# The last gates of a gated five-branch mixer layer: loading W_out's blocks in four groups between the gates, in a new order of steps

## The chip, the cores and the metric

One core of one Trainium2 chip runs the whole program. The metric is device microseconds of one execution, as the median of several runs of the same program. All data is float32 in device memory; a profiled execution gives the trace that the sections below read. Engines are named as the profile names them: PE (TensorE's matmuls), PEld (its weight loads), DVE (VectorE), ACT (ScalarE), POOL (GpSimd), SP (SyncE, which here only issues DMAs), and PEq, SPq, POOLq, ACTq for the queues that issue.

## The reference, cut to what matters

For 512 tokens of width 1024 a layer computes a normalised input, one wide projection of it, five branches of width 512, and merges them by gates:

```python
h = rmsnorm(x, norm_g)
proj = h @ w_in + b_in                 # branch inputs, and 5 x 1024 gate logits
y_a, y_b, y_c, y_d, y_m = ...          # five branches, each (512 tokens, 512)
gates = jax.nn.sigmoid(gate_logits).reshape(b, s, N_BRANCH, D_MODEL)
merged = jnp.zeros_like(x)
for n, y in enumerate((y_a, y_b, y_c, y_d, y_m)):
    merged = merged + gates[:, :, n] * (y @ w_up[n])
x = x + merged @ w_out
return rmsnorm(x, final_norm_g)
```

Branch D (number 3) is a gated linear recurrence over the tokens; it is the last to be finished here, so its gates and its up-projections end the merge, and the product with `w_out` (1024 x 1024), the residual and the last norm follow.

## The kernel before, in words

**Arithmetic.** Every large product is made of three matmuls (`mm3`, L196 to L201): both operands are split into a rounded part and a remainder (names ending in H or `hi`, and L or `lo`), and hi*hi, hi*lo and lo*hi are summed in one PSUM bank. One unit of 128 output channels with 1024 inputs is 8 x 3 = 24 matmuls of 128x512; one with 512 inputs is 12.

**Weights.** All weights come through one ring of two staging buffers, `wst` (`WST = 2`), of 512 KB each. `load_w` (L150) issues the load on SP's queue and splits it in two halves: `whi` by ACT (L162), `wlo` by DVE (L163). `load_w_add` (L171), used for the gates, makes `wlo` without DVE: ACT writes the negated rounded value (L182), POOL issues a DMA that reads the same weights from memory once more and adds them (L183), and ACT writes `whi` (L184). So each gate moves 512 KB on SP's queue and twice 256 KB on POOL's. `whi` and `wlo` have six halves each. A staging buffer is free for the next load when ACT (and DVE) have read it, and SP issues in order, so a load whose buffer is not yet free holds up every DMA behind it on SP.

**Steps.** The order of the work is written by hand in two strings, `STEPS` and `ENDS`, that a loop hands to `step(s)`. `G3` is one gate of branch D: a load, 24 matmuls, a sigmoid on ACT (L961). `U3` is one up-projection: 12 matmuls, then DVE multiplies by the gate (L975) and adds into `merged` (L977); one weight load serves two of them. `dt` and `dn` are D's tiles and its scan; `dn1` makes the last two of the four `y` tiles that every `U3` needs. There are eight `G3` and eight `U3`. Below, "gate 5" is the fifth `G3`, and so on. A scheduler then places each engine's instructions, so neighbouring steps overlap.

**W_out.** `merged @ w_out` is done by a scheme with fewer products: sums and differences of the blocks of `w_out` (`w0` to `w3`, in `weights(i)`, L1081) and of `merged`. `wout[half, k]` are the four blocks 11, 21, 12 and 22, each in two units `u` of 512 KB. In `ENDS` of the kernel before, `w0` loads both units of block 11 and `w1` both units of block 21 through `wst` and splits them (`operand`, L1059: `woH` by ACT, `woL` by DVE, both in `split_sb`, L218). `w2` and `w3` each handle one unit of the combined blocks: they load `t1` (block 12) into a buffer of its own, block 11 *again* through `wst` to subtract it (`minus`, L1065), `t2` (block 22) into a buffer of its own, subtract `t1`, and load block 21 *again* to subtract `t2` and split the result. So twelve 512 KB loads. `t1`, `t2`, `woH`, `woL` lie in `epool`, which takes the memory that the branches leave at `mid.close()`; the last reader there is D's scan.

**x's rows.** For the residual the first 256 tokens of `x` are loaded into buffers of the `y` tiles (`xr`, L1074), at the place in the program where `ENDS` begins.

**The last products.** Seven products follow (`product`, L1130), each two PSUM banks (one from pool `pj`, one from `at`). `take` (L1142) adds a bank to a row, `finish` (L1150) squares, normalises and stores. The last one, `b22` on the first 256 tokens, is done for tokens 0 to 127 in one piece of 512 columns and for tokens 128 to 255 in two pieces of 256 columns (`halves=(1, 2)`), both in one bank.

The whole order of the stretch is held by SP's queue, by the two staging buffers, and by ACT, DVE and POOL, which each work strictly in order.

Of the kernel before, what the change touches and what calls it, by code (L numbers as in the profile page):

```python
# [70 lines left out]
G4 U4 az3 an0 G4 G0 ao0 bv0 az2 az1 bp1 G0 ao2 ao3 ao1 ba2 U4 cv1 ba1 G0 U0 U4 ba0 U0 bv1 U0  # L71
G0 cg0 U0 bp2 ba3 G0 bp3 G1 ba6 ba4 ba5 U0 ba7 U0 G0 G0 U0 U0 G1 G1 cp0 G1 G1 cv0 cp2 ch0
U1 U1 G1 cp1 ds0 U1 U1 G1 U1 ch1 U1 G2 ch2 G1 cn0 G2 U1 cp3 G2 U1 ch3 G2 cn1 dt1 U2 dt0
U2 U2 dn0 G2 G3 G2 U2 U2 dt2 G2 U2 dt3 G3 G2 U2 G3 dn1
"""
ENDS = """
U2 G3 w0 G3 w1 G3 w2 G3 U3 w3 U3 U3 U3 G3 U3 U3 U3 U3
"""


def build(ctx, tc, x, mem, memT, cols_d, rows_d, wcm, wbv, wcv0, wcv1, wmk, wmv, wup, wout, dw, fg, out):
# [65 lines left out]
    def f32(t):  # L147
        return t.bitcast(F32)

    def load_w(src, n, scale=None, stage=wpool):  # L150

        st = stage.tile([P, 1056], F32, tag="wst", name="wst", bufs=WST)
        nc.sync.dma_start(out=st[:, :n], in_=src)
        res = []
        m = n // 2
        for half in range(2):
            hi = wpool.tile([P, 576], F32R, tag="whi", name="whi", bufs=WHL)
            lo = wpool.tile([P, 576], F32R, tag="wlo", name="wlo", bufs=WHL)
            f = st[:, half * m:(half + 1) * m]
            with tc.high_priority(offset=PREP):  # L160
                if scale is None:
                    act(hi[:, :m], f, AF.Copy)  # L162
                    V.tensor_tensor(out=lo[:, :m], in0=f, in1=f32(hi[:, :m]), op=ALU.subtract)  # L163
                else:
                    act(hi[:, :m], f, AF.Copy, scale=scale)
                    V.scalar_tensor_tensor(out=lo[:, :m], in0=f, scalar=scale, in1=f32(hi[:, :m]),
                                           op0=ALU.mult, op1=ALU.subtract)
            res.append((hi, lo))
        return res

    def load_w_add(src, n):  # L171

        st = wpool.tile([P, 1056], F32, tag="wst", name="wst", bufs=WST)
        nc.sync.dma_start(out=st[:, :n], in_=src)
        res = []
        m = n // 2
        for half in range(2):
# [805 lines left out]
    def step(s):  # L983
# [42 lines left out]
            assert None not in ys[i]  # L1026
            up(i, ys[i])
        elif c == "w":
            st[s] = weights(i)
        else:  # L1030
            raise ValueError(s)

# [17 lines left out]
    def block(half, k, u, tag="wst"):  # L1050
# [2 lines left out]
            t = wpool.tile([P, 1056], F32, tag="wst", name="wst", bufs=WST)[:, :D]  # L1053
        else:
            t = epool.tile([P, D], F32, tag=tag, name=tag, bufs=2)
        nc.sync.dma_start(out=t, in_=wout[half, 2 * k + u])
        return t

    def operand(f):  # L1059
# [10 lines left out]
    xr, sums, quarter = [], {}, {}  # L1070
    for t in range(2):
        xr.append([ypool.tile([P, S], F32, tag=f"y{n}", name=f"xr{t}{n}") for n in "HL"])
        for n in range(2):
            nc.sync.dma_start(out=xr[t][n], in_=x[t * P:(t + 1) * P, n * S:(n + 1) * S])  # L1074
    lo_t, hi_t = slice(0, H2), slice(H2, S)
    t1, t2, n4 = [], [], []

    def weights(i):
        if i < 2:
            return [operand(block(0, i, u)) for u in range(2)]  # L1080
        u = i - 2  # L1081
        t1.append(block(1, 0, u, "t1"))
        minus(t1[u], t1[u], block(0, 0, u))
        t2.append(block(1, 1, u, "t2"))
        minus(t2[u], t2[u], t1[u])
        f = block(0, 1, u)
        n4.append(operand(minus(f, f, t2[u])))

    for s in ENDS.split():
        step(s)  # L1090
    b11, b21 = st["w0"], st["w1"]
    hst.close()
    rpool = ctx.enter_context(tc.tile_pool(name="rpool", bufs=1, side="right"))
    s2H, s2L = (rpool.tile([P, 4, S], F32R, name=n) for n in ("s2H", "s2L"))
# [33 lines left out]
    def product(ps, a, sl, b, begin, halves=(1, 1), done=None):  # L1128

        for t in range(2):  # L1130
            tsl = slice(sl.start + t * P, sl.start + (t + 1) * P)
            w = S // halves[t]
            for c in range(halves[t]):
                cs = slice(c * w, (c + 1) * w)
                for j in range(4):
                    wh, wl = (v[:, (j % 2) * S + c * w:(j % 2) * S + (c + 1) * w] for v in b[j // 2])
                    ah, al = (v[:, j, tsl] for v in a)
                    mm3(ps[t][:, cs], [(ah, al, wh, wl)], first=begin and j == 0, last=j == 3, check=True)
                if done:
                    done(t, cs)  # L1140

# [72 lines left out]
    for t in range(2):  # L1214
        take(2 + t, 0, X[t])
        finish(2 + t, 0)
        take(2 + t, 1, X[t])
    Y = banks()
    product(Y, (s4H, s4L), hi_t, T1, True)
    for t in range(2):  # L1220
        take(2 + t, 1, Y[t])
        finish(2 + t, 1)

    def c12(t, cs):
        take(t, 1, Y[t], cs)
        finish(t, 1, cs)

    product(Y, (s4H, s4L), lo_t, b22, False, halves=(1, 2), done=c12)


def _layout(a):
# [56 lines left out]
```

## Time and profile before

| | us |
|---|---|
| median of 3 runs (860.98 to 866.45) | 862.5 |
| the profiled execution, its own time | 863.77 |
| its span in the profile | 862.1 |
| PE busy in the span | 829.0 |
| DVE busy | 601.7 |
| ACT busy | 499.6 |
| stretch between the last matmul of gate 4 and the first matmul of the `w_out` products | 742.2 to 812.97 |
| mean granted clock of the core | 0.987 |

The profile's lines are read so. The slice rows divide the span into 40 parts of 21.55 us; each digit is a share in tenths. A row of the timeline gives the start, the duration, the engine, the line, the operation, what it writes from what it reads, and in brackets how long its engine had been idle and what ended that. A matmul's duration is longer than its distance to the next, since matmuls are pipelined: the distance of two starts is the cost. The chain of waits in the end (PE 79%, issue 11%, DVE 4%, ACT 3%, DMA 2%) is PE for most of the program, so what PE waits for, and at what clock it runs, is what the end hangs on. DMA rows of a window give the count, the size and the median time from issue to landing.

### The profile page before, as it was taken

How to read it: one execution, taken by the hardware profiler on the slowest of the kernel's cores; microseconds unless marked ns; L12 is line 12 of the kernel's file. 1: busy time of each engine (PE TensorE's matmuls, PEld its weight loads, DVE VectorE, ACT ScalarE, POOL GpSimd, SP SyncE). 2: the span in 40 equal slices, each digit the busy share in tenths (PEclk: the TensorE clock that was granted, in tenths of full speed). 3: DMA queues.
4: the chain of work that ended last, by engine and by line, in shares of the span. 5: the costliest groups of instructions: out<-in, count | busy, mean ns of one | idle time of the engine just before them, and what ended most of it. 6: DMA issues, size and time to landing. Idle time of an engine off the chain costs nothing.

```text
span 862.1 us, 11382 instructions
## 1 busy us (share of the span) xinstructions
PE 829.0 (96%) x4028; PEld 697.3 (81%) x4028; DVE 601.7 (70%) x1136; ACT 499.6 (58%) x898; POOL 107.2 (12%) x159
## 2 busy tenths in 40 slices
PE   8999999999999999999999999999999999578995
PEld 7788888888898988888888988888888888356874
DVE  4879998997465597775647777487585645426796
ACT  6635475445645465666555464774659768633354
POOL 0000020101100241024322000110102011010010
PEclk9999999999999999999999999999999999879999
DMA  9442373544534333446534333652625456765232
GB/s 360 141 141 74 103 146 94 143 124 124 124 111 112 86 109 98 104 116 135 135 91 106 123 110 113 154 137 88 157 74 128 121 143 149 240 178 158 79 98 98
DMA packets 37712, 110.52 MB, mean 128 GB/s; under 512 B 4244, under 2 KB 4372, under 8 KB 37656
## 3 DMA queue, kind: packets, MB, share of 16 engines
q1 hardware_dynamic: 24952, 86.21, 30.2%
q0 software_dynamic: 11840, 22.03, 15.3%
q10 hardware_dynamic: 864, 1.57, 0.5%
q8 instruction: 31, 0.51, 0.2%
q14 instruction: 25, 0.20, 0.1%
HBM read 107.68 MB, written 2.11 MB: 127 GB/s over the span
## 4 chain that ended last, share of the span: by engine, by line
PE 79%; issue 11%; DVE 4%; ACT 3%; DMA 2%; POOL 1%; POOLq 0%; SPq 0%; ACTq 0%
PE pj L201 21%; PE pj L200 21%; PE pj L199 21%; DMA wlo<-in 2%; PE pj L530 2%; PE pj L529 2%; PE pj L528 2%; POOL wlo L183 1%; PE po L642 1%; PE wb L628 1%; PE og L833 1%; PE mk L286 1%; PE zb L599 1%; PE zb L598 1%; DMA mt<-in 1%
## 5 line engine op out<-in xcount | busy, mean ns | idle before, releaser
L201 PE MATMUL pj<-hH,wlo 128*128 128x512 f32 x768 | 303.0, 394 | 11.1 <-DMA wlo<-in 10.8
L199 PE MATMUL pj<-hH,whi 128*128 128x512 f32 x768 | 302.3, 394 | 8.4 <-ACT whi L184 8.4
L200 PE MATMUL pj<-hL,whi 128*128 128x512 f32 x768 | 302.1, 393 | 0.0
L162 ACT ACTIVATE whi<-wst 128x512 fp32r<-128x512 f32 (+1 forms) x172 | 106.9, 631 | 169.2 <-PE pj L200 117.3
L201 PEld LDWEIGHTS pj<-hH,wlo 128*128 128x128 f32 x768 | 145.7, 190 | 43.6 <-DMA wlo<-in 12.8
L199 PEld LDWEIGHTS pj<-hH,whi 128*128 128x128 f32 x768 | 145.8, 190 | 38.3 <-ACT whi L184 8.9
L200 PEld LDWEIGHTS pj<-hL,whi 128*128 128x128 f32 x768 | 145.9, 190 | 30.2
L163 DVE TENSOR_TENSOR wlo<-wst,whi 128x512 fp32r<-128x512 f32 (+1 forms) x172 | 116.9, 687 | 72.8 <-ACT whi L162 72.3
L183 POOL DMA_DIRECT2D wlo<-in x80 | 69.7, 885 | 587.8 <-ACT wlo L182 431.8
L416 DVE SCALAR_TENSOR_TENSOR acc<-u,cols,acc 128x512 f32<-128x512 f32 x120 | 88.6, 746 | 1.4
L184 ACT ACTIVATE whi<-wst 128x512 fp32r<-128x512 f32 x80 | 49.9, 628 | 55.0 <-PE pj L200 39.1
L200 PE MATMUL pj<-yL,whi 128*128 128x512 f32 x160 | 62.5, 390 | 0.0
L199 PE MATMUL pj<-yH,whi 128*128 128x512 f32 x160 | 62.4, 391 | 0.0
L201 PE MATMUL pj<-yH,wlo 128*128 128x512 f32 x160 | 62.2, 390 | 0.0
L182 ACT ACTIVATE wlo<-wst 128x512 fp32r<-128x512 f32 x80 | 49.1, 618 | 13.1 <-DMA wst<-in 7.2
L199 PEld LDWEIGHTS pj<-yH,whi 128*128 128x128 f32 x160 | 30.0, 188 | 6.3 <-ACT whi L162 0.2
L201 PEld LDWEIGHTS pj<-yH,wlo 128*128 128x128 f32 x160 | 30.0, 188 | 6.2
L200 PEld LDWEIGHTS pj<-yL,whi 128*128 128x128 f32 x160 | 30.1, 188 | 5.9
L618 DVE TENSOR_TENSOR_SCAN kp<-kp 128x512 f32<-128x512 f32 (+3 forms) x32 | 26.9, 859 | 10.8 <-POOL kp L611 10.6
L529 PE MATMUL pj<-wlo,hH 128*128 128x256 f32 (+1 forms) x112 | 31.8, 284 | 0.0
L530 PE MATMUL pj<-whi,hL 128*128 128x256 f32 (+1 forms) x112 | 31.8, 284 | 0.0
L528 PE MATMUL pj<-whi,hH 128*128 128x256 f32 (+1 forms) x112 | 31.5, 283 | 0.0
(388 smaller groups left out, 1259.1 us busy)
## 6 DMA issues: line engine op xcount, KB each, us to landing
wst<-in SPq DMA_DIRECT2D x140, 512.0 KB, 3.3
wlo<-in POOLq DMA_DIRECT2D x80, 256.0 KB, 5.5
xt<-in SPq DMA_DIRECT2D x4, 512.0 KB, 9.1
t<-in SPq DMA_DIRECT2D x4, 512.0 KB, 4.9
wst<-in SPq DMA_DIRECT2D x2, 528.0 KB, 4.2
mr<-in SPq DMA_DIRECT2D x2, 512.0 KB, 10.7
f<-crow SPq DMA_DIRECT2D x4, 256.0 KB, 6.9
merged<-in POOLq DMA_DIRECT2D x4, 256.0 KB, 3.8
```

The costliest lines, as they stand in the source:

```text
L162: act(hi[:, :m], f, AF.Copy)
L163: V.tensor_tensor(out=lo[:, :m], in0=f, in1=f32(hi[:, :m]), op=ALU.subtract)
L182: act(lo[:, :m], st[:, sl], AF.Copy, scale=-1.0)
L183: G.dma_start(out=lo[:, :m], in_=src[:, sl], accum_op=ALU.add)
L184: act(hi[:, :m], st[:, sl], AF.Copy)
L199: mm(ps, lhsT=ah, rhs=bh, start=first and i == 0, stop=False, skip_group_check=check)
L200: mm(ps, lhsT=ah, rhs=bl, start=False, stop=False, skip_group_check=check)
L201: end = mm(ps, lhsT=al, rhs=bh, start=False, stop=last and i == n - 1, skip_group_check=check)
L416: V.scalar_tensor_tensor(out=a, in0=u[:, k:k + S], scalar=col("a_w", i * 31 + k), in1=a, op0=ALU.mult, op1=ALU.add)
L528: mm(dst[t], lhsT=hH[:, k, tsl], rhs=wh, start=first, stop=False, skip_group_check=True)
L529: mm(dst[t], lhsT=hH[:, k, tsl], rhs=wl, start=False, stop=False, skip_group_check=True)
L530: mm(dst[t], lhsT=hL[:, k, tsl], rhs=wh, start=False, stop=k == NK - 1, skip_group_check=True)
```

## The change

It alters the order of a few steps, the way in which `w_out`'s blocks are loaded, the place of four loads of `x`, and the banks of the last product.

```diff
-U2 U2 dn0 G2 G3 G2 U2 U2 dt2 G2 U2 dt3 G3 G2 U2 G3 dn1
+U2 U2 dn0 G2 G3 G2 U2 U2 dt2 G2 U2 dt3 G2 U2 G3 U2 dn1
 """
 ENDS = """
-U2 G3 w0 G3 w1 G3 w2 G3 U3 w3 U3 U3 U3 G3 U3 U3 U3 U3
+G3 G3 w0 U3 G3 w1 U3 G3 w2 U3 G3 w3 U3 G3 U3 U3 U3 U3
 """
...
+    queued = [None]
+
     def load_w(src, n, scale=None, stage=wpool):
...
-        nc.sync.dma_start(out=st[:, :n], in_=src)
+        queued[0] = nc.sync.dma_start(out=st[:, :n], in_=src)
...
-        nc.sync.dma_start(out=t, in_=wout[half, 2 * k + u])
+        with tc.issue_after(queued[0].ins):
+            queued[0] = nc.sync.dma_start(out=t, in_=wout[half, 2 * k + u])
         return t
...
-        for n in range(2):
-            nc.sync.dma_start(out=xr[t][n], in_=x[t * P:(t + 1) * P, n * S:(n + 1) * S])
...
     def weights(i):
-        if i < 2:
-            return [operand(block(0, i, u)) for u in range(2)]
-        u = i - 2
-        t1.append(block(1, 0, u, "t1"))
-        minus(t1[u], t1[u], block(0, 0, u))
-        t2.append(block(1, 1, u, "t2"))
-        minus(t2[u], t2[u], t1[u])
-        f = block(0, 1, u)
-        n4.append(operand(minus(f, f, t2[u])))
+        u = i // 2
+        if i % 2 == 0:
+            f = block(0, 0, u)
+            t1.append(block(1, 0, u, "t1"))
+            b11.append(operand(f))
+            minus(t1[u], t1[u], f)
+        else:
+            t2.append(block(1, 1, u, "t2"))
+            minus(t2[u], t2[u], t1[u])
+            f = block(0, 1, u)
+            b21.append(operand(f))
+            n4.append(operand(minus(f, f, t2[u])))
 
     for s in ENDS.split():
         step(s)
-    b11, b21 = st["w0"], st["w1"]
+    with tc.issue_after(queued[0].ins):
+        for t in range(2):
+            for n in range(2):
+                nc.sync.dma_start(out=xr[t][n], in_=x[t * P:(t + 1) * P, n * S:(n + 1) * S])
...
-                    mm3(ps[t][:, cs], [(ah, al, wh, wl)], first=begin and j == 0, last=j == 3, check=True)
+                    alone = isinstance(ps[t], list)
+                    mm3((ps[t][c] if alone else ps[t])[:, cs], [(ah, al, wh, wl)],
+                        first=(begin or alone) and j == 0, last=j == 3, check=True)
...
+    take(1, 1, Y[1])
+    L = banks()
 
     def c12(t, cs):
-        take(t, 1, Y[t], cs)
+        take(t, 1, Y[0] if t == 0 else L[cs.start // H2], cs)
         finish(t, 1, cs)
 
-    product(Y, (s4H, s4L), lo_t, b22, False, halves=(1, 2), done=c12)
+    product((Y[0], L), (s4H, s4L), lo_t, b22, False, halves=(1, 2), done=c12)
```

Twelve loads of `w_out` blocks become eight: each unit of blocks 11 and 21 is staged once and used both for its own split and for the subtraction. A `U3` now stands after each of the groups `w0` to `w3`. `issue_after` keeps each block's load behind the load written before it. The four loads of `x` go behind the last weights of the `U3`. The last two 256-column pieces get a bank each, and the bank that they shared is added to the row beforehand in one go.

In the changed listing the same lines carry other numbers: L155 and L176 are the loads of `load_w` and `load_w_add` (before L153, L174), L164 and L165 their split (L162, L163), L184 and L186 the gate's copies (L182, L184), L1059 the blocks (L1056), L1101 the rows of `x` (L1074), L201 to L203 the three matmuls (L199 to L201). In the rows below `in_5` is the projection weights (here gates), `in_11` the up-projection weights, `in_12` `w_out`, `in_0` `x`.

**SP's queue, from the load of gate 4 on.** Before:

```order
L174 DMA wst_7218<-in_5 128x1024
L1056 DMA wst_7257<-in_12 128x1024
L1056 DMA wst_7263<-in_12 128x1024
L1074 DMA xr0H_7195<-in_0 128x512
L1074 DMA xr0L_7196<-in_0 128x512
L1074 DMA xr1H_7199<-in_0 128x512
L1074 DMA xr1L_7200<-in_0 128x512
L1056 DMA t1_7359<-in_12 128x1024
L1056 DMA t2_7364<-in_12 128x1024
L1056 DMA t1_7438<-in_12 128x1024
L174 DMA wst_7269<-in_5 128x1024
```

Between the loads of gate 4 (`wst_7218`) and gate 5 (`wst_7269`) stand two staged blocks, the four rows of `x` and three blocks for `t1` and `t2`. The changed kernel, from the same load on:

```order
L176 DMA wst_7214<-in_5 128x1024
L1059 DMA wst_7253<-in_12 128x1024
L155 DMA wst_7262<-in_11 128x1024
L176 DMA wst_7287<-in_5 128x1024
L1059 DMA t1_7255<-in_12 128x1024
L1059 DMA t2_7326<-in_12 128x1024
L1059 DMA wst_7329<-in_12 128x1024
L176 DMA wst_7355<-in_5 128x1024
L1059 DMA wst_7394<-in_12 128x1024
L1059 DMA t1_7396<-in_12 128x1024
L155 DMA wst_7403<-in_11 128x1024
L176 DMA wst_7428<-in_5 128x1024
```

Only one staged block and the first `U3` weights stand between gate 4's load and gate 5's (`wst_7287`) now; then `t1`, `t2` and a block stand before gate 6's (`wst_7355`), a block, a `t1` and `U3` weights before gate 7's (`wst_7428`). The built program's buffers: gate 5's load takes the buffer that the `U3` weights `wst_7262` leave, gate 6's that of the block `wst_7253`, gate 7's that of the block `wst_7394`, gate 8's that of gate 7.

**ACT, from D's last root on, to the copies of gate 5 before, to a block's copy ahead of gate 6 now.** `yH` is D's `y`, `woH` a block's rounded part, `g` a gate's sigmoid. Before:

```order
L939 ACTIVATE f_6989<-f_6989 128x512
L961 ACT_TABLE_LOAD
L961 ACTIVATE g_7154<-pj_7129,cols_80 128x512
L218 ACTIVATE yH_7169<-f_7158 128x512
L218 ACTIVATE yH_7176<-f_7161 128x512
L218 ACTIVATE woH_7259<-wst_7257 128x1024
L218 ACTIVATE woH_7265<-wst_7263 128x1024
L961 ACTIVATE g_7255<-pj_7230,cols_80 128x512
L182 ACTIVATE wlo_7272<-wst_7269 128x512
L182 ACTIVATE wlo_7277<-wst_7269 128x512
```

In the kernel before the two blocks' copies stand ahead of gate 5's. The changed kernel:

```order
L164 ACTIVATE whi_7264<-wst_7262 128x512
L164 ACTIVATE whi_7268<-wst_7262 128x512
L220 ACTIVATE yH_7152<-f_7137 128x512
L184 ACTIVATE wlo_7290<-wst_7287 128x512
L186 ACTIVATE whi_7289<-wst_7287 128x512
L184 ACTIVATE wlo_7295<-wst_7287 128x512
L186 ACTIVATE whi_7294<-wst_7287 128x512
L963 ACT_TABLE_LOAD
L963 ACTIVATE g_7212<-pj_7187,cols_80 128x512
L220 ACTIVATE woH_7257<-wst_7253 128x1024
L963 ACTIVATE g_7251<-pj_7226,cols_80 128x512
L220 ACTIVATE woH_7331<-wst_7329 128x1024
```

The first `U3`'s split (L164) now stands ahead of D's last `y`, gate 5's copies directly behind it, and the blocks' copies behind those; the block `wst_7329` is copied just ahead of gate 6's copies.

**PE, the end of the program.** Before, the two pieces of tokens 128 to 255 follow each other in one bank (`at_7898`), the last of the first piece and the first of the second being:

```order
L199 MATMUL at_7898<-woH_7849,s4H_7633 128x256
L200 MATMUL at_7898<-woL_7850,s4H_7633 128x256
L201 MATMUL at_7898<-woH_7849,s4L_7634 128x256
L199 MATMUL at_7898<-woH_7843,s4H_7633 128x256
L200 MATMUL at_7898<-woL_7844,s4H_7633 128x256
L201 MATMUL at_7898<-woH_7843,s4L_7634 128x256
```

The piece of tokens 0 to 127 (12 matmuls of 128x512) stands ahead of both. The changed kernel:

```order
L201 MATMUL pj_7950<-woH_7841,s4H_7625 128x256
L202 MATMUL pj_7950<-woL_7842,s4H_7625 128x256
L203 MATMUL pj_7950<-woH_7841,s4L_7626 128x256
L201 MATMUL at_7951<-woH_7835,s4H_7625 128x256
L202 MATMUL at_7951<-woL_7836,s4H_7625 128x256
L203 MATMUL at_7951<-woH_7835,s4L_7626 128x256
L201 MATMUL at_7951<-woH_7835,s4H_7625 128x256
L202 MATMUL at_7951<-woL_7836,s4H_7625 128x256
L203 MATMUL at_7951<-woH_7835,s4L_7626 128x256
L201 MATMUL pj_7889<-woH_7835,s4H_7625 128x512
```

The two pieces have banks of their own (`pj_7950`, `at_7951`), and the 12 wide matmuls of tokens 0 to 127 (`pj_7889`) stand between the halves of the second piece.

More of the change, by code (lines that the diff above doesn't have):

```diff
@@ L173, in load_w_add @@
         st = wpool.tile([P, 1056], F32, tag="wst", name="wst", bufs=WST)
-        nc.sync.dma_start(out=st[:, :n], in_=src)
+        queued[0] = nc.sync.dma_start(out=st[:, :n], in_=src)
         res = []
@@ L1028, in step @@
         elif c == "w":
-            st[s] = weights(i)
+            weights(i)
         else:
@@ L1072, in build @@
         xr.append([ypool.tile([P, S], F32, tag=f"y{n}", name=f"xr{t}{n}") for n in "HL"])
-        for n in range(2):
-            nc.sync.dma_start(out=xr[t][n], in_=x[t * P:(t + 1) * P, n * S:(n + 1) * S])
     lo_t, hi_t = slice(0, H2), slice(H2, S)
     t1, t2, n4 = [], [], []
+    b11, b21 = [], []
     def weights(i):
-        if i < 2:
-            return [operand(block(0, i, u)) for u in range(2)]
-        u = i - 2
-        t1.append(block(1, 0, u, "t1"))
-        minus(t1[u], t1[u], block(0, 0, u))
-        t2.append(block(1, 1, u, "t2"))
-        minus(t2[u], t2[u], t1[u])
-        f = block(0, 1, u)
-        n4.append(operand(minus(f, f, t2[u])))
+        u = i // 2
[10 more added lines that the diff above has]
+            n4.append(operand(minus(f, f, t2[u])))
     for s in ENDS.split():
         step(s)
-    b11, b21 = st["w0"], st["w1"]
+    with tc.issue_after(queued[0].ins):
+        for t in range(2):
+            for n in range(2):
+                nc.sync.dma_start(out=xr[t][n], in_=x[t * P:(t + 1) * P, n * S:(n + 1) * S])
     hst.close()
```

## The prediction

> **What bounds the kernel now.** I read the slices first, then the stretches, then PE's rows there, then the queues that feed it. Slices of PE and of the granted clock:
>
> ```profile
> PE   8999999999999999999999999999999999578995
> PEclk9999999999999999999999999999999999879999
> ```
>
> PE is full except in slices 35 to 37 (733 to 797 us), where the clock drops too. The stretches, with busy time and count per engine:
>
> ```profile
> core 0: us, PE busy (x) PEld busy (x) DVE busy (x) ACT busy (x) POOL busy (x), PEclk, DMA share, GB/s
> 742.20:813.00 70.80, 51.53 (x194) 40.33 (x194) 34.38 (x47) 25.88 (x43) 7.05 (x8) 0.86 0.60 178
> 813.00:855.00 42.00, 39.41 (x181) 32.00 (x179) 38.15 (x76) 21.07 (x39) 2.17 (x4) 1.00 0.17 53
> ```
>
> From gate 4 to the first product, DVE and ACT work half the time and DMA moves 178 GB/s. PE's rows, gate 4's first and last matmul, then every long wait:
>
> ```profile
> 736.76 0.39 PE L199 MATMUL pj<-hH,whi 128*128 128x512 f32 x1
> 741.97 0.39 PE L201 MATMUL pj<-hH,wlo 128*128 128x512 f32 x1
> 750.80 0.79 PE L199 MATMUL pj<-hH,whi 128*128 128x512 f32 x1 [8.43 <-ACT whi L184]
> 754.13 0.79 PE L201 MATMUL pj<-hH,wlo 128*128 128x512 f32 x1 [2.12 <-DMA wlo<-in]
> 766.13 0.50 PE L201 MATMUL pj<-hH,wlo 128*128 128x512 f32 x1 [3.38 <-DMA wlo<-in]
> 767.18 0.63 PE L199 MATMUL pj<-hH,whi 128*128 128x512 f32 x1
> 777.53 0.79 PE L201 MATMUL pj<-hH,wlo 128*128 128x512 f32 x1 [4.05 <-DMA wlo<-in]
> 797.42 0.50 PE L201 MATMUL pj<-hH,wlo 128*128 128x512 f32 x1 [1.28 <-DMA wlo<-in]
> 812.97 0.39 PE L199 MATMUL pj<-woH,aH 128*128 128x512 f32 x1
> ```
>
> 23 steps from 736.76 to 741.97 are 0.2266 us each. Four gates and eight up-projections are 192 matmuls, 43.5 us; the stretch 742.2 to 812.97 takes 70.8. So 27.3 us are lost: 19.3 in the five waits, the rest at the low clock (0.63 us rows) that follows them. All five wait for a gate's weights. Why these are late:
>
> ```profile
> 736.27 0.33 SPq L1074 DMA_DIRECT2D xr0H<-in  x1
> 741.65 1.28 SPq L1056 DMA_DIRECT2D t<-in  x3
> 744.06 0.33 SPq L174 DMA_DIRECT2D wst<-in  x1
> 740.88 0.69 DVE L218 TENSOR_TENSOR yL<-f,yH 128x512 fp32r<-128x512 f32 x1 [0.16 <-ACT yH L218]
> 749.08 1.15 ACT L182 ACTIVATE wlo<-wst 128x512 fp32r<-128x512 f32 x2 [4.89 <-DMA wst<-in]
> 750.00 1.75 POOL L183 DMA_DIRECT2D wlo<-in  x2 [17.93 <-ACT wlo L182]
> ```
>
> x's rows stood at SP's head until the last U2 had read the y tiles; `t1` stood until D's last `yL` (740.88 + 0.69) left its memory; gate 5's load, behind both, went at 744.06. Load, copy, POOL's DMA and its landing follow in a row: 5.0 us, 0.9 us, and 4.1 us to PE at 754.13.
>
> **The change part by part.** *Steps.* `STEPS` only swaps what is ready: by 742.2 PE has done the same gates and all U2 in both orders, and the gates' data is there early. U3 1 needs D's last y. On ACT one table load fewer stands ahead of it and two weight splits more, on DVE two remainders more:
>
> ```profile
> 730.15 0.62 ACT L182 ACTIVATE wlo<-wst 128x512 fp32r<-128x512 f32 x1
> 735.49 1.28 ACT L939 ACT_TABLE_LOAD   x1
> 776.54 1.15 ACT L162 ACTIVATE whi<-wst 128x512 fp32r<-128x512 f32 x2 [2.78 <-DMA wst<-in]
> 777.20 1.29 DVE L163 TENSOR_TENSOR wlo<-wst,whi 128x512 fp32r<-128x512 f32 x2 [5.36 <-ACT whi L162]
> ```
>
> So its `yL` ends at 741.57 - 1.28 + 1.15 + 1.29 = 742.7. U3 1 uses it only in its last matmuls, after 744: no wait. Its weights load when gate 4's are copied (730.8), long before.
>
> *Gate 5.* Its buffer is the one of those weights, whose second remainder stands four DVE/ACT steps (2.6 us) ahead of `yL`: load at 740.1. I need the prices of DMAs in this traffic: count, size, median to landing in 740 to 800, then least, median and most of the staged loads (700 to 840), of `t` and of `wlo` (740 to 800):
>
> ```profile
> wst<-in SPq DMA_DIRECT2D x15, 512.0 KB, 5.1
> t<-in SPq DMA_DIRECT2D x4, 512.0 KB, 4.9
> wlo<-in POOLq DMA_DIRECT2D x8, 256.0 KB, 6.7
> DMA to landing us min/median/max: 3.1/4.5/6.9
> DMA to landing us min/median/max: 3.6/4.9/5.9
> DMA to landing us min/median/max: 4.1/6.7/8.1
> 771.40 1.76 POOL L183 DMA_DIRECT2D wlo<-in  x2 [9.13 <-ACT wlo L182]
> ```
>
> For PE the first half counts: 4.1 us after POOL began at 750.00, 6.1 after 771.40; I take 5.0. Gate 5's load is almost alone (`t1` goes only after 742.7), so 3.5: landed 743.6, POOL 744.5, PE 749.5. PE has finished U3 1 at 744.9 and idles about 4 us, then is cold once: 8 matmuls at 0.43 instead of 0.23, 1.6 us (the rows from 767.18 do that).
>
> *Gates 6 to 8* hang on a chain through the two buffers. Prices of its links, an ACT copy of a block, its DVE remainder and the subtraction; a gate's four copies are 1.15 + 1.13, 2.2:
>
> ```profile
> 751.68 1.06 ACT L218 ACTIVATE woH<-wst 128x1024 fp32r<-128x1024 f32 x1 [0.42 <-DMA wst<-in]
> 752.77 1.23 DVE L218 TENSOR_TENSOR woL<-wst,woH 128x1024 fp32r<-128x1024 f32 x1 [7.60 <-ACT woH L218]
> 764.34 1.23 DVE L1066 TENSOR_TENSOR t<-t,wst 128x1024 f32<-128x1024 f32 x1 [3.77 <-DMA wst<-in]
> 750.13 1.13 ACT L184 ACTIVATE whi<-wst 128x512 fp32r<-128x512 f32 x2
> ```
>
> - `t1` waits for `yL`: 742.75, + 4.9 = 747.65. Subtraction and remainder free the first block's buffer: + 2.46 = 750.1.
> - Gate 6's load: + 5.1 = 755.25; copied 757.45; to PE 755.25 + 0.9 + 5.0 = 761.2. PE, from 749.5, has 34 matmuls (7.7, + 1.6 cold) and two more: idle at 759.2, 2.0 us.
> - The next block's load waits for that copy: 757.5 + 5.1 = 762.6; copy, remainder, subtraction 3.5: 766.1.
> - Gate 7's load: 766.2 + 5.1 = 771.3; copied 773.5; to PE 777.2. In between PE does U3 3 and 4, with waits of about 1.5 (U3 3's remainder stands behind the subtraction on DVE, 768.2), 2.4 (gate 7's first rounded half, ahead of U3 4 in PE's order, 772.9) and 1.1.
> - Gate 8's load takes gate 7's buffer: 773.6 + 5.1 = 778.7; to PE 784.6; idle 1.9.
> - 22 matmuls (5.0) and U3 5 to 8 (48, 10.9), whose weights are there: 800.5.
>
> So the first product starts at 800.5 instead of 812.97: **-12.5 us**. Idle falls from 27.3 to some 14.5; what is late next is still gates, through blocks. Four loads fewer (2 MB) are in these links already. x's rows cost nothing: they stand behind the last U3 weights, which load from 780.9 on (gate 8 copied), and DVE wants them 12 matmuls into the products, at 803; without that cover the first `take` would wait their 5 us.
>
> The low clock: the 1.28 wait left it high (0.39 us rows after 797.42), the 3.38 one did not. My waits of 1.1 to 2.4 lie nearer the first; I take no cold phase after them, 6.4 us for four as the upper end. The Trainium skill ("TensorE: Matmul & The Clock Gate", "Part 1: The HAM clock gate") has the half clock after an idle window of about 3.4 us, which would spare them; by it the sum stays. The row shows 3.38 already enough, and no run here shows 2 us alone.
>
> *The last pieces.* The shared bank cost a wait:
>
> ```profile
> 853.26 0.39 PE L199 MATMUL at<-woH,s4H 128*128 128x256 f32 x1 [1.86 <-DVE xr1L L1146]
> 854.67 0.28 PE L201 MATMUL at<-woH,s4L 128*128 128x256 f32 x1
> 858.61 0.34 ACTq L1186 DMA_DIRECT2D out<-xr1L  x1
> ```
>
> With a bank each PE goes on: -1.86. From PE's last matmul to the last store's issue were 3.7 us; in the new order the row of tokens 0 to 127 ends late too, and its square (0.7 us on ACT) stands between: about +0.35. The extra `take` of the whole bank, one DVE row of 0.68, runs under 36 matmuls. **-1.5 us.** The five products between are the same work, so 42 us.
>
> Sum: -14.0. On the profiled execution: span 862.1 to 848.1, its time 863.77 to 849.8. The median of the runs shown is 1.3 under that execution: 862.5 - 14.0 = **848.5 us**.
>
> Bounds: with the least landings (t 3.6, four staged loads 3.1, `wlo` 4.1) the chain is 10.2 shorter, 838.3; with the most (5.9, 6.9, 6.1 for the first half) 9.3 longer, 857.8. I give 841 to 858, most links being independent.
>
> **The rivals.**
>
> 1. *Landing is cheap once less is loaded.* For: four loads and the burst at 741 to 745 are gone, and from 690 to 740 the staged loads took less:
>
> ```profile
> wst<-in SPq DMA_DIRECT2D x7, 512.0 KB, 3.7
> ```
>
> Against: gates, blocks and POOL's second reads still share the stretch. All at the least: 838. The Trainium skill ("DMA: Bandwidth & Descriptors", "Anatomy of one DMA") puts a DMA at 2.0 us plus bytes / 436e3, an estimate of 3.2 us for 512 KB; the least row, 3.1, agrees, the median, 5.1, does not. By 3.2 for each staged load this forecast would be 841.
>
> 2. *The chain through the buffers eats most of it.* Each block stands between two gates' loads; with the longest landings and the four cold phases, -14.0 + 9.3 = -4.7, 857.8, and up to 864 cold: no change that can be told.
> 3. *Blocks ahead of gates on ACT and in the buffers set the pace* (slower). Gate 6's and 8's copies stand behind a block's on ACT. If each of gates 6 to 8 had to wait out a block (6.9 + 3.5) and its own load and copies (6.9 + 2.2), 19.5 per gate: from 751.1, gate 8's load at 790, PE at 803, first product 819, + 4.5 cold: 823.5; 862.5 + 10.5 - 1.5 = 871.5. It decides where the links average over 6.5 us and gate 8's load also falls behind its block. Against: the block ahead of gate 8 does not hold its buffer.
> 4. *The change doesn't reach the end*: PE's gain is given back in 813 to 855, where DVE is busy 38.15 of 42. For: DVE paces the products. Against: its work there is unchanged and starts as much earlier; PE would wait at most for the block splits moved into it, none. 855 to 860, within rival 2's chance.
>
> **How the numbers follow.** Forecast 0.62, rival 1 0.15, rivals 2 and 4 0.18, rival 3 0.05. Over 1% (8.6 us, about what a measurement of this kernel tells from no change) means under 853.9 or over 871.1. Rival 1 and nearly all of the forecast are faster: 0.78; rivals 2, 4 and a rest: 0.18; slower 0.04.
>
> **What would show it.** Right: no 8 us wait at gate 5 but one of about 4, waits of 1 to 3 us at gates 6 to 8, gate 5's load issued near 740, `t1` near 743, the first product near 800, no wait before the last piece. Wrong: a gate waiting over 5 us, SP held at a block while a gate's load stands behind, cold rows after every short wait, or DVE's waits in the products growing.

## The result and the profile after

| | before | after |
|---|---|---|
| median of the comparison, us (4 runs each) | 863.5 (861.0 to 866.5) | 853.6 (853.0 to 857.5) |
| profiled execution, its span, us | 863.77, 862.1 | 853.64, 851.7 |
| first product's first matmul, us | 812.97 | 800.44 |
| from there to the span's end, us | 49.1 | 51.3 |

The ratio is 0.989 with a 95% interval of 0.985 to 0.994: 10.0 us faster, where 14.0 were forecast (848.5 us, a ratio of 0.984, just outside the interval; the measured 853.6 lies inside the stated range of 841 to 858). A second comparison of the same two kernels gave 0.988 (0.985 to 0.992).

The stretches of the changed kernel, with the columns of the first windows above:

```profile
742.20:803.00 60.80, 51.16 (x206) 39.08 (x205) 34.62 (x49) 27.03 (x44) 7.02 (x8) 0.94 0.64 186
803.00:845.00 42.00, 38.13 (x170) 30.99 (x168) 37.51 (x75) 22.07 (x40) 2.17 (x4) 0.96 0.21 73
```

The first of these windows ends 2.6 us inside the products, so it holds 206 matmuls where the one of before holds 194. From gate 4 to the first product it is 58.2 us (742.2 to 800.44) in place of 70.8. DMA moves 186 GB/s in place of 178. In the products the work is the same, but the clock is 0.96 where it was 1.00. The waits of PE, and the first product:

```profile
747.85 0.79 PE L201 MATMUL pj<-hH,whi 128*128 128x512 f32 x1 [2.64 <-ACT g L963]
750.26 0.79 PE L203 MATMUL pj<-hH,wlo 128*128 128x512 f32 x1 [1.19 <-DMA wlo<-in]
764.41 0.50 PE L203 MATMUL pj<-hH,wlo 128*128 128x512 f32 x1 [1.21 <-DMA wlo<-in]
782.91 0.50 PE L203 MATMUL pj<-hH,wlo 128*128 128x512 f32 x1 [1.83 <-DMA wlo<-in]
787.15 0.50 PE L203 MATMUL pj<-hH,wlo 128*128 128x512 f32 x1 [1.20 <-DMA wlo<-in]
800.44 0.39 PE L201 MATMUL pj<-woH,aH 128*128 128x512 f32 x1
824.88 0.50 PE L202 MATMUL pj<-woL,s4H 128*128 128x512 f32 x1 [1.87 <-DVE woL L220]
```

The five waits of 8.4 to 1.3 us have become these and four under 0.8, 9.7 us in all up to the first product in place of 19.3; the wait before the last piece (1.86) is gone, and one of 1.87 stands in the sixth product. The loads of gates 5 to 8 and the first two of t (`t1` and `t2`) on SP:

```profile
740.32 0.33 SPq L176 DMA_DIRECT2D wst<-in  x1
742.97 0.80 SPq L1059 DMA_DIRECT2D t<-in  x2
750.02 0.33 SPq L176 DMA_DIRECT2D wst<-in  x1
765.86 0.33 SPq L176 DMA_DIRECT2D wst<-in  x1
771.54 0.33 SPq L176 DMA_DIRECT2D wst<-in  x1
```

Gate 5's load goes 3.7 us earlier than before (744.06), and ahead of t1. Gate 8's, 17.4 us earlier than before (788.93). What holds gate 8 now is read on ACT and POOL:

```profile
777.92 1.15 ACT L184 ACTIVATE wlo<-wst 128x512 fp32r<-128x512 f32 x2 [4.88 <-DMA wst<-in]
778.84 1.76 POOL L185 DMA_DIRECT2D wlo<-in  x2 [6.83 <-ACT wlo L184]
```

From the issue of the load to the copy are 6.4 us, from there to POOL 0.9, from POOL to PE's first use 4.1 and to its second 8.3 (782.91, 787.15).

### The profile page after: what moved, and what is told of

Same layout as the page of the kernel before. It is cut to its first block, busy times and chain, and to the rows that moved or that the text cites. A ratio compares the mean times of both kernels' runs of the same rounds, so it can differ in the third digit from the quotient of the medians.

```text
span 851.7 us, 11377 instructions
## 1 busy us (share of the span) xinstructions
PE 827.2 (97%) x4028; PEld 695.2 (82%) x4028; DVE 601.5 (71%) x1137; ACT 498.9 (59%) x897; POOL 106.6 (13%) x159
## 3 DMA queue, kind: packets, MB, share of 16 engines
q10 hardware_dynamic: 864, 1.57, 0.5%
## 5 line engine op out<-in xcount | busy, mean ns | idle before, releaser
L203 PE MATMUL pj<-hH,wlo 128*128 128x512 f32 x768 | 301.3, 392 | 5.9 <-DMA wlo<-in 5.6
L201 PE MATMUL pj<-hH,whi 128*128 128x512 f32 x768 | 300.7, 392 | 3.3 <-ACT g L963 2.6
L164 ACT ACTIVATE whi<-wst 128x512 fp32r<-128x512 f32 (+1 forms) x172 | 106.8, 630 | 160.3 <-PE pj L202 113.0
L203 PEld LDWEIGHTS pj<-hH,wlo 128*128 128x128 f32 x768 | 144.7, 188 | 38.3 <-DMA wlo<-in 8.0
L201 PEld LDWEIGHTS pj<-hH,whi 128*128 128x128 f32 x768 | 144.8, 189 | 33.3 <-ACT g L963 3.1
L165 DVE TENSOR_TENSOR wlo<-wst,whi 128x512 fp32r<-128x512 f32 (+1 forms) x172 | 117.0, 687 | 71.2 <-ACT whi L164 70.9
L186 ACT ACTIVATE whi<-wst 128x512 fp32r<-128x512 f32 x80 | 50.0, 628 | 55.9 <-PE pj L202 40.0
L201 PE MATMUL pj<-yH,whi 128*128 128x512 f32 x160 | 62.5, 392 | 0.4 <-ACT g L963 0.4
L203 PE MATMUL pj<-yH,wlo 128*128 128x512 f32 x160 | 62.5, 390 | 0.3 <-DVE wlo L165 0.3
L184 ACT ACTIVATE wlo<-wst 128x512 fp32r<-128x512 f32 x80 | 49.2, 619 | 15.9 <-DMA wst<-in 10.0
L203 PEld LDWEIGHTS pj<-yH,wlo 128*128 128x128 f32 x160 | 30.1, 188 | 7.0 <-DVE wlo L165 0.8
L201 PEld LDWEIGHTS pj<-yH,whi 128*128 128x128 f32 x160 | 30.1, 188 | 6.9 <-ACT g L963 0.8
```

Of the source, the lines that this page charges most:

```text
L184: act(lo[:, :m], st[:, sl], AF.Copy, scale=-1.0)
L186: act(hi[:, :m], st[:, sl], AF.Copy)
L201: mm(ps, lhsT=ah, rhs=bh, start=first and i == 0, stop=False, skip_group_check=check)
L203: end = mm(ps, lhsT=al, rhs=bh, start=False, stop=last and i == n - 1, skip_group_check=check)
```

## The experiments

All are compared with the kernel before on the same chip. "Start" is the first product's first matmul in the profile, "rest" the time from there to the span's end, a difference of rounded figures that is good to 0.1 us. The kernel before has 812.97 and 49.1.

| kernel | ratio (95%) | start | rest |
|---|---|---|---|
| changed, once more | 0.988 (0.985 to 0.992) | 801.0 | 49.7 |
| e1 changed, last pieces in one bank | 0.987 (0.984 to 0.989) | 804.5 | 49.4 |
| e2 before, banks alone | 1.000 (0.998 to 1.002) | 811.8 | 50.0 |
| e3 before, steps alone | 1.001 (0.999 to 1.003) | 814.0 | 48.7 |
| e4 changed, twelve loads | 1.001 (1.000 to 1.003) | 815.5 | 49.3 |
| e5 changed, blocks in own buffers | 0.985 (0.983 to 0.988) | 801.0 | 49.5 |
| e6 changed, row 0 first | 0.988 (0.985 to 0.990) | 802.2 | 50.8 |
| e7 e6 and late finish | 0.986 (0.984 to 0.989) | 802.2 | 49.5 |
| e8 changed, x's rows early | 0.991 (0.988 to 0.994) | 804.3 | 49.7 |
| e9 changed, no second reads | 0.975 (0.973 to 0.978) | 792.3 | 49.8 |
| e10 e5, gate 8 early | 0.979 (0.976 to 0.982) | 792.5 | 53.7 |
| e11 e10 and e9's edit | 0.973 (0.971 to 0.976) | 787.4 | 52.8 |

**The changed kernel once more.**

> The changed kernel as it is, once more. My theory: its first product starts 12.5 us earlier than in the kernel before, 3.6 us of this are given back behind it: a wait of 1.9 us before the second matmul of the sixth product (DVE's remainder of block 12 is 1.2 us later, because the normalising of tokens 128 to 255 now stands ahead of it on DVE), one cold phase after that wait (1.6), and a tail 1.4 longer. These come from the order of instructions, so they return: 853.5, within 1 us, first product at 800.4, the same wait. Rival: the give-back is chance (one cold phase, late landings); then the median lies at 851 to 852 and the wait is away in another profile.

The wait of 1.87 in the sixth product came back, the low clock behind it did not. The same place in the first profile, then in this one:

```profile
826.03 0.63 PE L203 MATMUL pj<-woH,s4L 128*128 128x512 f32 x1
826.46 0.63 PE L201 MATMUL pj<-woH,s4H 128*128 128x512 f32 x1
```

```profile
825.45 0.50 PE L202 MATMUL pj<-woL,s4H 128*128 128x512 f32 x1 [1.87 <-DVE woL L220]
825.79 0.39 PE L203 MATMUL pj<-woH,s4L 128*128 128x512 f32 x1
826.02 0.40 PE L201 MATMUL pj<-woH,s4H 128*128 128x512 f32 x1
```

Steps of 0.43 against 0.23: eight of them are the 1.6 us by which the rest of 51.3 differs from 49.7. So of the 3.6 us that I took for a give-back (14.0 forecast, a span 10.4 shorter), 1.6 is chance. The median was 856.0 here, outside what both expectations gave; but the kernel before took 865.4 beside it, so the two are 9.3 apart. So kernels of different comparisons are set side by side by their ratios.

**e1, the bank edit undone.** In the last product

```diff
-    product((Y[0], L), (s4H, s4L), lo_t, b22, False, halves=(1, 2), done=c12)
+    product(Y, (s4H, s4L), lo_t, b22, False, halves=(1, 2), done=c12)
```

with the extra `take` and `L` gone.

> The changed kernel with the two last pieces in one bank again, and the extra addition of the bank gone. My theory: the edit on the banks is worth about nothing, since it takes a wait of 1.86 us away and puts the pieces of tokens 0 to 127 near the end, which lengthens the tail by 1.4: this kernel takes 854.0, within 1 us of the changed one, has the wait of 1.9 before the last piece again, a tail of 3.7 from PE's last matmul to the last store, and still the 1.9 before the sixth product. Rival, the prediction's term: the edit is worth 1.5, and this kernel takes 855.0 or more.

No worse than the changed kernel; the rest is 49.4, with the wait back (1.10 us here) and a tail of 3.3 us from PE's last matmul (ended 846.9) to the last store's issue (850.23). In both profiles of the changed kernel the tail is 4.8. So in the changed kernel the edit takes away 1.1 us of wait and adds 1.5 of tail. The first product is late here (804.5): one gate waited 2.9 us, with slow matmuls behind it, in a stretch that the edit doesn't touch.

**e2, the bank edit alone** (the same lines put into the kernel before).

> The kernel before with only the edit on the banks. My theory: gain 1.86 less a tail 1.4 longer, so 0.5 us faster than the kernel before, not to be told from it; no wait before the last piece. Rival: 1.5 us faster or more. A third: the give-back behind the first product (wait and cold phase before the sixth product) comes with this edit, then this kernel is 1 to 3 us slower than the kernel before.

Worth nothing: 1.000. The wait is gone and PE needs 39.8 us for the products in place of 42.0 (first matmul to the end of the last, 811.81 to 851.65), but the tail is 5.7 in place of 3.7. What ACT does from PE's end on (some short rows left out):

```profile
851.58 0.60 ACT L1162 ACTIVATE junk<-xr0L 128x512 f32<-128x512 f32 x1 [1.09 <-DVE xr0L L1148]
852.54 0.37 ACT L1162 ACTIVATE junk<-xr1L 128x256 f32<-128x256 f32 x1
852.93 0.71 ACT L1187 ACTIVATE merged<-merged,rs 128x512 f32<-128x512 f32 x1
853.55 0.36 ACT L1162 ACTIVATE junk<-xr1L 128x256 f32<-128x256 f32 x1
854.09 0.72 ACT L1187 ACTIVATE merged<-merged,rs 128x512 f32<-128x512 f32 x1
855.44 0.71 ACT L1187 ACTIVATE xr0L<-xr0L,rs 128x512 f32<-128x512 f32 x1
856.57 0.72 ACT L1187 ACTIVATE xr1L<-xr1L,rs 128x512 f32<-128x512 f32 x1 [0.42 <-DVE rs L1183]
857.32 0.34 ACTq L1188 DMA_DIRECT2D out<-xr1L  x1
```

PE ends earlier, but at that point all four rows still have to be scaled and two of them squared, and ACT does it one after the other: two scalings of `merged`, the square of row 0 and its scaling stand among those of the last piece.

**e3, the order of steps alone**: the two strings, with gate 5 ahead of the first blocks.

> The kernel before with only the order of steps changed: the last two gates of the first string and the last U2 in the new order, gate 5 written ahead of the first blocks; the twelve loads, x's rows and the banks as before. My theory: nothing, because gate 5's load still stands on SP behind x's rows and behind the loads of t1 and t2, which wait for D's last remainder: its issue stays at 744 to 745, the first product at 811 to 814, 863 within 2 us. Rival: it is the order of the steps that pays; then gate 5's load goes at 740, and the kernel takes 855 to 858.

As expected, nothing: gate 5's load went at 744.03, on SP behind x's rows and all four t. The t's had been issued by 743.5; the last 0.5 us it waited for its staging buffer, which the first block held until DVE had made its remainder (744.02).

**e4, twelve loads.**

```diff
         if i % 2 == 0:
-            f = block(0, 0, u)
+            b11.append(operand(block(0, 0, u)))
             t1.append(block(1, 0, u, "t1"))
-            b11.append(operand(f))
-            minus(t1[u], t1[u], f)
+            minus(t1[u], t1[u], block(0, 0, u))
```

and the same for `b21`.

> The changed kernel with its new order of steps, x's rows last and a bank each, but each unit of blocks 11 and 21 is loaded twice again, once for its split and once for the subtraction: twelve loads in place of eight. My theory: the second load of block 11 and t1, which waits for D's last remainder at 742.7, now stand on SP ahead of U3's and gate 5's loads, and three more 5 us links lie in the chain through the two staging buffers; gate 5's load goes after 748, the first product starts at 812 or later, and the kernel is no faster than the kernel before (ratio 0.995 to 1.01). Rival: the order of the steps and the place of x's rows make the gain, and the four loads saved are hidden anyway; then the ratio stays within 0.986 to 0.991.

As expected, the whole gain is gone (1.001). SP, up to gate 6's load, and the instruction of DVE that let gate 5's load go:

```profile
741.72 0.33 SPq L1059 DMA_DIRECT2D t<-in  x1
742.10 0.42 SPq L1059 DMA_DIRECT2D wst<-in  x1
744.03 0.33 SPq L155 DMA_DIRECT2D wst<-in  x1
748.25 0.33 SPq L176 DMA_DIRECT2D wst<-in  x1
...
756.82 0.33 SPq L176 DMA_DIRECT2D wst<-in  x1
747.00 1.23 DVE L1069 TENSOR_TENSOR t<-t,wst 128x1024 f32<-128x1024 f32 x1 [3.00 <-DMA wst<-in]
```

Gate 5's load goes at 748.25, gate 6's at 756.82, 8 and 7 us later than in the changed kernel. Gate 5's load took the staging buffer into which block 11 had been loaded a second time, and went when DVE's subtraction had read it (747.00 to 748.23). The run doesn't separate the four loads from the place of gate 5's load behind t1, which they bring with them. No run has the eight loads with the old order of steps, so what the eight loads are worth without the new order is not shown.

**e5, blocks in own buffers.** The blocks that a group splits are loaded into buffers of `t2` and `t1` that the next groups need only later, so that the ring `wst` serves gates and up-projections alone (the last group excepted):

```diff
-            f = block(0, 0, u)
-            t1.append(block(1, 0, u, "t1"))
+            f = block(0, 0, u, f"t2{u}")
+            t1.append(block(1, 0, u, f"t1{u}"))
...
-            f = block(0, 1, u)
+            f = block(0, 1, u, *([] if u else ["t11"]))
```

> The changed kernel, but the blocks 11 and the first block 21 are loaded into the buffers of t2 and t1 that are not in use yet, so that the ring of two staging buffers serves gates and U3 weights alone (but for one block at the end); no more memory, the same eight loads. Theory of the prediction (the chain through the staging buffers sets gates 6 to 8): gate 6's load goes at about 741 to 743 in place of 750, PE waits about 4 us at gate 5 as before and nearly nothing at gates 6 to 8, and the first product starts at 793 to 796 in place of 800.4 to 801: 5 to 7 us less than the changed kernel, ratio 0.980 to 0.984. Rival: the landings set the pace (what is in flight together lands later, POOL's second reads above all); then the waits for wlo stay, the first product starts at 799 to 802, ratio 0.987 to 0.990.

Half of it held. PE's waits from gate 5 to gate 7 shrank to 2.3 us in all; the last of them, and then gate 8:

```profile
764.98 0.50 PE L203 MATMUL pj<-hH,wlo 128*128 128x512 f32 x1 [0.29 <-DMA wlo<-in]
780.09 0.80 PE L201 MATMUL pj<-hH,whi 128*128 128x512 f32 x1 [7.10 <-ACT whi L186]
```

```profile
750.05 21.10 SPq L1059 DMA_DIRECT2D t<-in  x4
771.25 0.38 SPq L1059 DMA_DIRECT2D wst<-in  x1
771.68 0.42 SPq L176 DMA_DIRECT2D wst<-in  x1
```

The last gate's load stood behind five blocks on SP and went at 771.68, against 771.54 in the changed kernel; the first product started at 801.0, as there. What is spared ahead of the last gate turns into a wait at it. My theory for the loss in this stretch (the ring) was too narrow: it is the ring or, with that gone, SP's order. The ratio of 0.985 lies some 3 us below the changed kernel's 0.988, but the two intervals overlap, and the profile shows no gain in the stretch.

**e6 and e7, the products.** e6 does the piece of tokens 0 to 127 ahead of both others; e7 also holds the squaring and scaling of tokens 128 to 255 behind block 12's remainders:

```diff
-    product((Y[0], L), (s4H, s4L), lo_t, b22, False, halves=(1, 2), done=c12)
+    end = product((Y[0], L), (s4H, s4L), lo_t, b22, False, halves=(1, 2), done=c12, rows=(0,))
+    with tc.issue_after(end.ins):
+        product((Y[0], L), (s4H, s4L), lo_t, b22, False, halves=(1, 2), done=c12, rows=(1,))
...
     with behind(s4_end):
         T1 = [operand(f) for f in t1]
+    with behind(split_end[0]):
+        finish(1, 0)
```

> The changed kernel, but in the last product the piece of tokens 0 to 127 is done before both pieces of tokens 128 to 255, in their own banks. Theory: the tail of 5.0 us from PE's last matmul to the last store comes from two rows that end together, so that ACT and DVE finish both in a row; here the first row is finished under the 24 matmuls that follow, no wait comes back, and the tail is 3.7 as in the kernel before: 1.3 us less than the changed kernel, ratio 0.986 to 0.988 in the same company, and the tail in the profile. Rival: DVE is busy with the row of tokens 384 to 511 there anyway; then the piece of tokens 0 to 127 waits for its bank and the gain is below 0.5, tail over 4.4.

> As the one before, and the squaring and scaling of tokens 128 to 255's first half is held behind DVE's remainders of block 12. Theory: these two instructions (0.75 us) stand ahead of the remainder that the sixth product waits for; held back, the wait of 1.87 falls to 0.7 to 1.1, as in the kernel before, and 0.7 to 1.2 us less than the kernel with only the new last order: ratio 0.984 to 0.987. Rival: DVE's whole queue is late there because the operand sums came later, not because of these two; then the wait stays at 1.5 or more and the time is the same.

e6: the tail fell to 4.2 us (last matmul ended 844.82, last store issued 849.04), between the two expectations; the wait in the sixth product was there, with the low clock behind it again. e7: that wait fell from 1.88 to 1.21, but PE then waited 0.66 for DVE at the start of the last product, and the rest, 49.5, is that of the changed kernel without its low clock, 49.7. Neither edit moves the time by what it takes away on PE.

**e8, x's rows early**: the four loads at their old place in the program.

> The changed kernel with the four loads of x's rows written at their old place, ahead of the last steps; on SP they now stand behind gate 5's load and ahead of t1. My theory, and the prediction's step: x's rows cost nothing where they stand; the rows go at about 741 to 742, t1 a little later, the first product stays at 800 to 804, ratio 0.986 to 0.990. Rival: 1 MB more at 742 makes t1, t2 and the first blocks land later; then first product at 805 or later, ratio over 0.991.

0.991 (0.988 to 0.994) fits both expectations. Gate 6's load went at 752.39 in place of 750.02 and the first product started at 804.3; other profiles of the changed order start at 800.4 to 804.5. What the place of x's rows is worth stays open: some 2 us by the two ratios, but their intervals overlap.

**e9, no second reads.**

```diff
-        w = load_w_add(wcm[CM_INDEX[c]], D) if c >= GATES else load_w(wcm[CM_INDEX[c]], D, scale)
+        late = c >= GATES + 3 * D + 4 * P and c < GATES + 4 * D
+        w = load_w_add(wcm[CM_INDEX[c]], D) if c >= GATES and not late else load_w(wcm[CM_INDEX[c]], D, scale)
```

> The changed kernel, but the weights of gates 5 to 8 are split as those of the up-projections are: ACT writes the rounded half, DVE the remainder; POOL's two reads of 256 KB per gate are gone (2 MB less), DVE has four times 1.3 us more. Theory: what PE waits for at gates 5 to 8 is the copy, POOL's issue and the landing of the second read, 6 to 7 us behind the load; with the remainder on DVE it is 1.3 to 2, so the waits for wlo and the cold phase of 1.6 behind the first go: first product at 794 to 797 in place of 800.4 to 802.2, ratio 0.980 to 0.984. Rival: the loads themselves come late, since each waits for a staging buffer behind a block, and DVE's remainders now stand behind the blocks' work; then gains under 2 us, ratio 0.986 to 0.990.

More than expected: 0.975, and a first product at 792.3. All waits of PE that are left before it:

```profile
746.75 0.50 PE L201 MATMUL pj<-hH,whi 128*128 128x512 f32 x1 [1.70 <-ACT g L964]
762.00 0.50 PE L201 MATMUL pj<-yH,whi 128*128 128x512 f32 x1 [1.33 <-ACT whi L164]
763.76 0.50 PE L203 MATMUL pj<-yH,wlo 128*128 128x512 f32 x1 [1.03 <-DVE wlo L165]
```

None is at gates 6 to 8. The loads land sooner as well. DMA of 740 to 800 (packets, MB, share of 16 engines; then issues and median us to landing), first the changed kernel, then e9:

```profile
q1 hardware_dynamic: 2880, 9.44, 45.2%
q0 software_dynamic: 1152, 2.10, 21.2%
wst<-in SPq DMA_DIRECT2D x12, 512.0 KB, 4.5
wlo<-in POOLq DMA_DIRECT2D x8, 256.0 KB, 6.4
```

```profile
q1 hardware_dynamic: 2880, 9.44, 44.0%
wst<-in SPq DMA_DIRECT2D x12, 512.0 KB, 3.4
```

The second reads were 2.1 MB beside 9.4, but a third of the engines' busy time; without them a staged load takes 3.4 us in place of 4.5. The run takes away two things at once, the second reads' traffic and the chain of copy, POOL and landing that PE waited for; it doesn't tell their shares apart.

**e10 and e11.** e10 is e5 with w2 behind gate 7 and the fourth `U3`, and w3 behind gate 8; e11 adds e9's edit.

```diff
-G3 G3 w0 U3 G3 w1 U3 G3 w2 U3 G3 w3 U3 G3 U3 U3 U3 U3
+G3 G3 w0 U3 G3 w1 U3 G3 U3 G3 w2 U3 G3 w3 U3 U3 U3 U3
```

> The kernel with the blocks in their own buffers, and in the last string the group w2 stands behind gate 7 and the fourth U3, and w3 behind gate 8. With own buffers alone the waits at gates 5 to 7 were gone (0.15 to 1.5 us), but gate 8's load stood on SP for 21 us behind block loads that waited for their buffers (issued 771.7, PE waited 7.1, then 1.7 and one cold phase). Theory: it is now the order on SP alone that holds gate 8; here only blocks with free buffers stand ahead of its load, it goes at 756 to 762, PE waits under 2 us at gate 8, the first product starts at 790 to 794: ratio 0.976 to 0.981. Rival: gate 8's weights are late for another reason (the six halves that gate 6 must give back, POOL's reads); then the wait stays over 4 and the ratio at 0.985.

> The kernel with own buffers and gate 8 early, and the weights of gates 5 to 8 split by ACT and DVE without the second reads. Theory: both causes are taken away and what is left in the stretch is the wait at gate 5 (about 2 us, for a bank that ACT's sigmoid frees late); the first product starts at 788 to 791, ratio 0.974 to 0.979. Rival: DVE, with four splits more and the blocks pushed towards the end, becomes the bound, and the remainders of blocks or the operand sums come late: the waits move into the products, ratio 0.981 or more.

e10: gate 8's load went at 759.42, PE's rows show no wait at gates 6 to 8, and the first product starts at 792.5, as forecast for SP's order. But the rest grew from 49.5 to 53.7: PE waited 3.43 us for DVE's remainder of block 12 in the sixth product (818.46), and eleven slow matmuls followed. e11 starts at 787.4, within 1.7 us of PE's bare work (742.2 + 43.5), and gives 3 us back:

```profile
813.39 0.79 PE L202 MATMUL pj<-woL,s4H 128*128 128x512 f32 x1 [3.49 <-DVE woL L221]
```

```profile
787.35:840.10 52.75, 40.61 (x181) 33.04 (x179) 44.29 (x94) 24.77 (x45) 2.17 (x4) 0.91 0.23 80
```

DVE works 44.3 us there, against 42.3 in the changed kernel: the wait for its remainder of block 12 is 3.5 and the clock falls behind it. So both expectations for e11 hold in part: the stretch is all but empty (0.8 us of waits), and the wait has moved to DVE in the products, though the ratio is not the 0.981 or more that went with it. e11 is the fastest of all, 842.3 against 865.6, e9 with its two lines 843.9; between these two the intervals overlap.

## Why the prediction was right, and what was mis-sized

- **What bounded the kernel, and the cause** (gates' loads held up by other loads): right, and shown by e4, which puts loads back ahead of the gates and loses all. e3 (steps) and e2 (banks) gain nothing alone, so the gain is the eight loads in their new order; x's rows may add some 2 us (e8, not told from nothing). One reading was not exact. That gate 5's load stood "behind both", x's rows and `t1`, is so, but neither was what it waited for last: SP had issued the third t by 742.93, then stood idle 1.0 us, until DVE's remainder had freed the first block's staging buffer (744.04). SP's waits in 743 to 745 us of the kernel before (who waited for whom, total, times, longest):

```profile
SPq L174 <- DVE woL L218: 1.0, 1, 1.0
```

  The loads of gates 6 to 8 (754.02, 765.59, 788.93) also went within 0.02 us after DVE had freed their buffer. So the two staging buffers bound the gates' loads in the kernel before too, and a block staged twice takes one of them twice.
- **Steps, and D's last y:** right. The order of steps alone is worth 0, and the last `yL` ended at 742.89 (742.7 forecast).
- **Gate 5:** load 740.32 (740.1), waits 2.64 and 1.19 (about 4 in one), one phase at the low clock. But the first of the two waits was ended by ACT: the sigmoid that frees a bank stood behind gate 5's copies and a table load. I had looked for weights alone.
- **The chain for gates 6 to 8:** issues at 750.02, 765.86 and 771.54 against 750.1, 766.2 and 773.6; first product 800.44 against 800.5. So close a hit is partly luck: the five profiles in which this stretch is the changed kernel's (the first, its repeat, e1, e6, e7) start at 800.4, 801.0, 804.5, 802.2 and 802.2, on average 802.1; the two that have the stretch of before (the profile shown and e2) at 813.0 and 811.8, on average 812.4. That is -10.3 where the sum has -12.5, so this term was 2.2 too large; one profile of each kernel could not have told, since the five differ by 4.1 among themselves. And e5 shows that the ring is not the only thing that holds the loads: SP's order takes its place.
- **"The low clock ... I take no cold phase after them":** right in this stretch in the first profile, where single waits of 1.2 and 1.8 us left the clock high, but not in general: e6 and e7 had slow matmuls behind a wait of 1.57 (last section).
- **The step that failed is "-1.86 ... about +0.35. -1.5 us."** The wait went, as said, but the tail grew by 2.0 (e2), or by 1.5 in the changed kernel (4.8 against e1's 3.3), not by 0.35, and the edit is worth 0 within 0.2%. I counted one square of row 0 that stands between; the runs showed that with PE out of the way ACT and DVE still have four rows to finish, in which PE's gain disappears. e6 and e7 show the same on a smaller scale. Rival 4 had the idea (PE's gain given back behind the first product, where DVE is busy), but looked for it in the splits of blocks, not in the tail; in e10 and e11 PE did wait for such a split.
- **"The five products between are the same work, so 42 us":** the same work, in another order. Two instructions for tokens 128 to 255 (L1181 and L1186, `finish`), which stood behind block 12's first remainder on DVE, now stand ahead of it. After, and then before:

```profile
817.00 0.15 DVE L1181 TENSOR_SCALAR v<-ss 128x1 f32<-128x1 f32 x1
817.07 0.68 DVE L1186 TENSOR_TENSOR xr1H<-xr1H,rows 128x512 f32<-128x512 f32 x1
...
823.60 1.22 DVE L220 TENSOR_TENSOR woL<-t,woH 128x1024 fp32r<-128x1024 f32 x1
```

```profile
834.93 1.22 DVE L218 TENSOR_TENSOR woL<-t,woH 128x1024 fp32r<-128x1024 f32 x1
...
836.13 0.68 DVE L1174 TENSOR_TENSOR xr1H<-xr1H,rows 128x512 f32<-128x512 f32 x1
```

  The remainder comes 23.2 us behind the first product in place of 22.0, hence the wait of 1.87 in place of 0.68. The two instructions explain 0.7 of the 1.2 us: e7, which holds them back, has 1.21. Where the other half comes from is not shown. It costs little time: unless slow matmuls follow the wait, the rest is 49 to 50 us with it or without.
- **The sum:** -10.3 for the stretch, about 0 behind it, against a measured -10.0.
- **Rivals 1, 2 and 3** did not come. But e9 says that rival 1 named a real price: with the second reads gone a staged load takes 3.4 us, near the least of 3.1, and the stretch gives 8 to 10 us more. The section of the Trainium skill that the prediction cites there ("DMA: Bandwidth & Descriptors", "Anatomy of one DMA") gives its fit for DMAs issued from GpSimd, while the staged loads are issued on SP's queue.

## What to carry to other kernels

Where one queue issues all loads in order, list what stands ahead of each load that PE waits for, when that can go, and whose buffer the load takes; loading a block once, with the gate's load ahead of `t1` and the later blocks, was worth all of the gain here, while the same steps without it were worth nothing. Where a stretch is bound by landings, look first at reads of the same bytes a second time: leaving out 2 MB of them was worth as much again as the whole change. And where DVE is almost as busy as PE (38 of 42 us) and ACT has rows left to finish after PE's last matmul, a wait taken away on PE came back in the tail, so the price of such an edit is worked out on the engines that finish the rows.

## What the hardware showed that I had not expected

- **Accumulating DMAs are dear.** In 740 to 800 us of the changed kernel the POOL queue's adds took 21.2% of the 16 engines' time for 2.10 MB, the plain loads 45.2% for 9.44 MB: 10.1 against 4.8% per MB, 2.1 times as much per byte. The size of the packets is not the reason: the adds go in packets of 2 KB and the weights in packets of 4 KB, but the 512 plain packets of 2 KB in the same stretch (x's rows) took 84 ns each at the median, the adds' 1024 took 178 ns, and a plain packet of 4 KB 159. In landing time the difference is less plain: 256 KB of adds, issued in pairs, landed in 6.4 us where 512 KB of weights took 4.5, but x's rows of 256 KB, issued four in a row, took 5.7 to 6.0.
- **Short waits cool PE by chance.** Over all fourteen profiles, every wait of PE of 2.9 us or more was followed by matmuls at 0.43 us a step. Of sixteen waits of 1.5 to 2.0 us, with none of 1 us in the 5 us before, four were, too: the wait of 1.87 or 1.88 in the sixth product was in the first profile and in e6's, not in the repeat's, e1's or e8's. Of single waits of 1.0 to 1.5 none was; two in a row in e9 (1.33 and 1.03) were. Of waits between 2.0 and 2.9 with no second one close by, that of 2.46 in e4 was, that of 2.14 in e8 was not. So, as an estimate from four of sixteen at 1.6 us each, a wait of 1.5 to 2.0 us costs some 0.4 us besides itself, which moves runs of one kernel apart. The Trainium skill ("TensorE: Matmul & The Clock Gate", "Part 1: The HAM clock gate") has a free-running activity window of about 3.4 us and calls the count of slow matmuls run-variable. That the same wait cools PE in one execution and not in another agrees; 2.9 and even 1.6 us being enough is less than its idle window.
